# Pinning the first MLP blocks in order, splitting the last weights into dead tiles, and two moved products in a one-layer encoder kernel

## The chip, the cores and the metric

The kernel runs as one program on one core of a Trainium2 chip. The metric is device time of one launch, in microseconds (us), as the median of the runs shown. A core has five engines that each work through their own queue of instructions: TensorE (PE, with its weight loads shown apart as PEld), VectorE (DVE), ScalarE (ACT), GpSimd (POOL) and SyncE (SP), which issues nearly all DMAs here. They wait for each other through semaphores. The order of each queue is fixed when the program is built.

## The reference

One encoder layer over 256 tokens of width 2048, in float32. Only the last two parts bear on the change:

```python
h = rms_norm(x, norm_x_g[l]); mem_n = rms_norm(mem, norm_mem_g[l])
x = x + cross_attention(h, mem_n, w_xq[l], w_xkv[l], w_xo[l])      # ends in "... @ w_o"
h = rms_norm(x, norm_ffn_g[l])
x = x + jnp.square(jax.nn.relu(h @ w_ff1[l])) @ w_ff2[l]           # 2048 -> 8192 -> 2048
return rms_norm(x, norm_final_g)
```

## The kernel before

**Products in three parts.** A float32 operand is split into a high part, rounded to the fast matmul type (tiles `whi`, `whx` for weights, the first of a pair `q` for activations), and the rest (`wlo`, `wlx`). A product is high times high, high times low and low times high. Each 1 MB piece of weights goes through the same steps: a DMA from the SP queue into `raw` (three buffers), ACT copies half of it to the high tile (line 125), DVE subtracts to get the low tile (line 126), PE multiplies. There are three buffers of `whi` and `wlo`. From the MLP on, every fourth half goes into a fourth pair, `whx` and `wlx`, which lies in memory that the cross attention has given up and holds one buffer.

**Blocks.** A block (`blocks`, `blocks_in_steps`) makes 256 columns of a projection: it takes two pieces of weights and so four halves, a quarter of the depth each. A quarter is 16 matmuls: eight at line 210 (high half times both parts of the activations, 512 columns) and eight at line 211 (low half, 256 columns), into two banks of PSUM, `s0` and `s1` (two buffers each). At its end ACT and DVE add the parts up (`bo`, lines 220 and 221) and hand them to the caller.

**The end of the attention.** `residual_pass` multiplies by `w_xo` in eight blocks and adds to `rt`, the residual stream by features; it also collects the sum of squares in `acc2`. Its first two blocks are interleaved by quarters with `values()` of the last head, by a written list of which block takes the next step. When the eighth block is done, two tiny matmuls (line 1043) sum `acc2` over the partitions, DVE makes the mean of it (line 1045), POOL the inverse root (line 267), and DVE transposes the whole of `rt` into `tr` with four instructions (line 1123), so that it can be placed token by token into `res` by DMAs (`place`, line 1130).

**The MLP.** It runs in four parts of 2048 hidden columns (`fb` 0 to 3). Each part has a first projection, eight blocks of `w_ff1`, and a second, `with_seven`, which multiplies by 2048 rows of `w_ff2`; half of that is done with seven products in place of eight, on sums of tokens (`summed`) and of weights (`b11` to `b22`, loaded whole into the memory of `rt` and `tr`). Parts 1 to 3 are `early`: some of the seven products are made between blocks of the first projection. `read` notes a finished bank of PSUM that is to be added to `res`; `read_now` does so when the next product or `plain` piece starts (line 1141), and in the last part it also squares the sums for the final norm and multiplies by its gain (`settle`, line 1153). `product` splits its weights itself (lines 1234 and 1235) and may then overwrite one of the four weight tiles with a difference (line 1239).

**What sets the order.** A scheduler lays the instructions of each engine when the program is built, from priorities and a time model of its own. `issue_after` ties an instruction behind another. In parts 1 to 3 every quarter of a block is tied behind the one before it through the list `ends`; in part 0 it is not, and `None` is passed.

Of the kernel before, what the change touches and what calls it, by code (L numbers as in the profile page):

```python
# [18 lines left out]
D = 2048  # L19
# [33 lines left out]
def trunk(ctx: ExitStack, tc: tile.TileContext, x_f, mem_f, positions, lead_f, small_f, w_in, ret_gn_g, w_out, w_xq,  # L53
# [13 lines left out]
    def stream_ps():  # L67
        s0 = psp.tile([P, 512], F32, name="s0", tag="s0", bufs=2)
        s1 = psp.tile([P, 512], F32, name="s1", tag="s1", bufs=2)
        return s0, s1  # L70
# [8 lines left out]
    def half_tiles():  # L79

        turn[0] += 1
        if spare and turn[0] % 4 == 0:
            return tuple(spare[0].tile([P, 1024 + room], F32R, name=nm, tag=nm, bufs=1)
                         for nm, room in (("whx", 128), ("wlx", 0)))
        return tuple(wp.tile([P, 1024 + room], F32R, name=nm, tag=nm, bufs=3) for nm, room in (("whi", 64), ("wlo", 0)))
# [924 lines left out]
    def residual_pass(quads, w, gain, name, loader=None, between=None):  # L1010
        nxt = []
        acc = xa.tile([P, S], F32, name="acc2", tag="acc2", bufs=2)
        vec.memset(acc, 0.0)
        first_two = []
        for b2 in range(8):
            xc = loader(b2) if loader else None
            if b2 % 2 == 0:
                nxt.append(quad_b())

            def evac(b, ps, b2=b2, xc=xc):  # L1020
                k = 2 * b2 + b
                vec.tensor_add(rt[:, k, :], ps, xc[:, b, :] if loader else rt[:, k, :])
                g = gains[:, gain + k:gain + k + 1]
                qh, ql = (a[:, k % 4, :] for a in nxt[-1])
                act.activation(qh, rt[:, k, :], AF.Copy, scale=g)
                vec.scalar_tensor_tensor(ql, rt[:, k, :], g, qh.bitcast(F32), op0=ALU.mult, op1=ALU.subtract)
                sq = xa.tile([P, S], F32, name="sq2", tag="sq2", bufs=2)
                act.activation(sq, rt[:, k, :], AF.Square)
                vec.tensor_add(acc, acc, sq)

            if not between or b2 > 1:
                blocks(quads, w, b2 * 256, 2, evac)
                continue
            first_two.append(blocks_in_steps(quads, w, b2 * 256, 2, evac))
            if b2:
                for which in (0, 0, 0, None, 1, 0, 0, 1, 1, 1, 1):
                    if which is None:
                        between()
                    else:
                        next(first_two[which], None)  # L1040
        ps = bank()
        for t in range(NT):
            pe.matmul(ps[:, 2 * t:2 * t + 2], acc[:, t * P:(t + 1) * P], ones[:, :2], start=True, stop=True)
        s = sm.tile([P, NT], F32, name=f"{name}_s", tag="rc_s")
        vec.tensor_scalar(s, ps[:, 0:4:2], 1.0 / D, EPS, op0=ALU.mult, op1=ALU.add)
        r = cp.tile([P, NT], F32, name=f"{name}_r")
        rsqrt(r, s)
        return nxt, r
# [100 lines left out]
    def settle(n, t):  # L1149

        got = res[:, t, n * 512:(n + 1) * 512]
        square_sum(ssq4[:, t, (0, 1, 3, 2)[n]:(1, 2, 4, 3)[n]], got)
        vec.tensor_mul(got, got, final[0][:, n * 512:(n + 1) * 512])

    def mean_square(t):
        s = sm.tile([P, 1], F32, name="s4", tag="s4")
        vec.tensor_reduce(s, ssq4[:, t, 0:4], axis=AX.X, op=ALU.add)
        vec.tensor_scalar(s, s, 1.0 / D, EPS, op0=ALU.mult, op1=ALU.add)
        sums.append(s)
# [25 lines left out]
    def with_seven(hid, rows, last, early):  # L1185
# [3 lines left out]
        own = {}  # L1189
# [9 lines left out]
        def read(*those):  # L1199

            reads.extend(those)

        def read_now():
            for n, t, ps, *done in reads:
                add_later(n, t, ps)
                if last and done:
                    settle(n, t)
            reads.clear()

        def triple(o, lhs, rhs, key, last=False):  # L1210
# [13 lines left out]
                                 [a[:, i % 2, :] for a in halves[i // 2]], (n, t), q == 3 and i == 3)  # L1224
            ends.append(ins)

        def product(o, lhs, raw, key, then=None):


            halves = []  # L1230
            with tc.high_priority(offset=100000):
                for c in range(0, 2048, 1024):
                    hi, lo = (h[:, :1024] for h in half_tiles())
                    latest["hi"] = act.activation(hi, raw[:, c:c + 1024], AF.Copy).ins  # L1234
                    latest["lo"] = vec.tensor_sub(lo, raw[:, c:c + 1024], hi.bitcast(F32)).ins  # L1235
                    halves.append([a.rearrange("p (k n) -> p k n", n=512) for a in (hi, lo)])
                for c in range(0, 2048, 1024) if then else ():
                    with tc.issue_after(latest["lo"]):
                        vec.tensor_sub(*(a[:, c:c + 1024] for a in then))
            read_now()  # L1240
            for oc, k, c0, c1 in ([(a[:, :256], (key, c), c * 256, c * 256 + 256) for c, a in enumerate(o)]
                                  if isinstance(o, tuple) else [(o, key, 0, 512)]):
                for i in range(4):
                    ins = triple(oc, lhs(i), [a[:, i % 2, c0:c1] for a in halves[i // 2]], k, i == 3)
                ends.append(ins)

        def part(b, t):
            return lambda i: [a[:, 2 * (i % 2) + b, t * P:(t + 1) * P] for a in hid[i // 2]]

        def summed(j):  # L1250
            return lambda i: [a[:, i, j * P:(j + 1) * P] for a in s_hl]
# [5 lines left out]
        if early:  # L1257
# [13 lines left out]
            yield  # L1271
            product(shared, summed(2), b12, "shared", (b11, b21, b11))
            read((0, 1, shared), (1, 1, shared))
            yield
            for n in range(2):
                take(n, stream_ps())
# [2 lines left out]
            if last:  # L1279
                final.append(quad_a().both.rearrange("p k s -> p (k s)").bitcast(F32))  # L1280
                with tc.issue_after(fetched[-1]):
                    nc.sync.dma_start(final[0], norm_final_g.partition_broadcast(P))
            product(own[1][0], summed(3), b22, (1, 0))
            plain(0, 3)
            load_block(b22, 1, 3)
            product(own[0][0], part(1, 0), b21, (0, 0))
# [22 lines left out]
            read((3, 0, own[3][0], True), (3, 1, own[3][1]))  # L1309
            product(own[2][0], part(1, 0), b21, (2, 0))  # L1310
            read((2, 0, own[2][0], True))
            if last:
                read((2, 1, own[2][1]))
            product(shared, summed(2), b12, "shared")
            if last:
                mean_square(0)
                finish_row(0)
            read((2, 1, shared), (3, 1, shared, True))
            if not last:
                product(own[2][1], part(1, 1), b11, (2, 1))  # L1320
                read((2, 1, own[2][1]))
            else:
                ends_of = stream_ps()
                product(ends_of, part(1, 1), b11, "end")
                for c, ps in enumerate(ends_of):
                    got = add(2, 1, ps[:, :256], c * 256, c * 256 + 256)
                    junk = sm.tile([P, 512], F32, name="junk", tag="junk", bufs=1)
                    acc = ssq4[:, 1, 3 + c:4 + c]
                    vec.scalar_tensor_tensor(junk[:, :256], got, 1.0, got, op0=ALU.mult, op1=ALU.mult, accum_out=acc)
                    if c:  # L1330
                        vec.scalar_tensor_tensor(sums[1], acc, 1.0 / D, sums[1], op0=ALU.mult, op1=ALU.add)
                    else:
                        mean_square(1)
                finish_row(1)
# [40 lines left out]
    for fb in range(4):  # L1375
        hid = []
        rows = w_ff2[0, fb * D:(fb + 1) * D, :]
        early = fb > 0
        parts_of = with_seven(hid, rows, fb == 3, early)
        ends.clear()  # L1380
        for b2 in range(8):
            hs = fp.tile([P, 2, S], F32, name="hs", tag="hs", bufs=2)
            if b2 % 2 == 0:
                hid.append(quad_a())

            def evac_h(b, ps):
                if early:
                    act.activation(ps, ps, AF.Relu)
                    act.activation(hs[:, b, :], ps, AF.Square)
                else:  # L1390
                    vec.scalar_tensor_tensor(hs[:, b, :], ps, 0.0, ps, op0=ALU.max, op1=ALU.mult)
                qh, ql = (a[:, b2 % 2 * 2 + b, :] for a in hid[-1])
                act.activation(qh, hs[:, b, :], AF.Copy)
                vec.tensor_sub(ql, hs[:, b, :], qh.bitcast(F32))
                if b2 < 4 and b:
                    token_sums(b2, hs)

            blocks(h3, w_ff1[0], fb * D + b2 * 256, 2, evac_h, ends if early else None)
            if early and b2 > 2:
                next(parts_of)  # L1400
            if fb == 0:
                place(b2)
        for _ in parts_of:
            pass
# [42 lines left out]
```

## Time and profile before

| | |
|---|---|
| median of 3 runs | 2046.75 us (2046.49 to 2047.02) |
| profiled execution, its own time | 2046.86 us |
| its span, first to last instruction | 2045.2 us |
| mean granted TensorE clock | 0.999 |
| PE busy | 2033.4 us (99%) |
| DVE busy | 1550.1 us (76%) |
| ACT busy | 1185.1 us (58%) |
| DMA queue with the weights (q1) | 402.74 MB, 61.2% of 16 engines |

All times inside the profile are counted from the start of the span. The time of the run is 1.7 us longer than the span. PE's busy time covers nearly all of it, so the few places in which PE stands still, and the stretch behind its last matmul, are what a change of order can win or lose. In the views below a row of the timeline gives the start, the time taken, the engine, the line and operation, the tile written and those read, and, in brackets, how long the engine stood idle before it and which instruction ended that.

### The profile page before, as it was taken

The numbers are of one execution on the slowest core, as the hardware profiler recorded it, in microseconds if no ns is written. First come the engines' busy times: TensorE is split into PE (matmuls) and PEld (weight loads), VectorE is DVE, ScalarE is ACT, GpSimd is POOL, SyncE is SP. The second block draws the span as 40 slices with busy tenths as digits, with TensorE's granted clock in tenths as the row PEclk, the third lists the DMA queues.
The fourth block names the chain that finished last, engine by engine and source line by source line (L and its number), as shares of the span: only waits on it lengthen the run. The fifth ranks groups of instructions, "written<-read, shape, count | busy, mean of one in ns | idle before, by whom it ended". The sixth has DMA issues, their size and how long they took to land.

```text
span 2045.2 us, 28450 instructions
## 1 busy us (share of the span) xinstructions
PE 2033.4 (99%) x10802; PEld 1751.9 (86%) x10802; DVE 1550.1 (76%) x2422; ACT 1185.1 (58%) x1941; POOL 39.8 (2%) x50
## 2 busy tenths in 40 slices
PE   9999999999999999999999999999999999999998
PEld 7888888988888888888888899888888888888886
DVE  5887788779667875888567666777867887888788
ACT  6665764575457555755455555555546656656655
POOL 0000000000000000000000000000000000000000
PEclk9999999999999999999999999999999999999999
DMA  9689556455555655555467655569657646655761
GB/s 330 210 259 301 187 182 200 151 194 197 178 168 185 201 183 165 193 182 182 164 217 232 191 180 161 175 180 246 233 167 232 220 164 213 201 204 165 242 232 62
DMA packets 329225, 405.24 MB, mean 198 GB/s; under 512 B 34928, under 2 KB 239360, under 8 KB 328960
## 3 DMA queue, kind: packets, MB, share of 16 engines
q1 hardware_dynamic: 328656, 402.74, 61.2%
q8 instruction: 84, 1.38, 0.3%
q10 hardware_dynamic: 432, 0.69, 0.1%
q14 instruction: 53, 0.43, 0.1%
HBM read 389.74 MB, written 11.55 MB: 196 GB/s over the span
## 4 chain that ended last, share of the span: by engine, by line
PE 98%; DVE 1%; DMA 0%; ACT 0%; issue 0%; SPq 0%; POOLq 0%; POOL 0%; ACTq 0%
PE s L210 34%; PE s L211 18%; PE s L167 8%; PE s L168 8%; PE s L166 8%; PE s L1213 7%; PE b L1213 7%; PE s L403 1%; PE s L401 1%; PE s L402 1%; PE b L796 1%; PE b L699 1%; PE b L829 1%; PE b L138 0%; PE b L137 0%; PE b L139 0%
## 5 line engine op out<-in xcount | busy, mean ns | idle before, releaser
L210 PE MATMUL s<-q,whi 128*128 128x512 f32 x2816 | 973.3, 391 | 0.8 <-DVE bo L221 0.6
L126 DVE TENSOR_TENSOR wlo<-raw,whi 128x1024 fp32r<-128x1024 f32 x584 | 712.7, 1221 | 298.5 <-ACT whi L125 294.1
L125 ACT ACTIVATE whi<-raw 128x1024 fp32r<-128x1024 f32 x584 | 618.8, 1060 | 499.3 <-PE s L210 208.8
L211 PE MATMUL s<-q,wlo 128*128 128x256 f32 x2816 | 768.9, 281 | 0.0
L210 PEld LDWEIGHTS s<-q,whi 128*128 128x128 f32 x2816 | 520.7, 188 | 103.4 <-DVE bo L221 0.9
L211 PEld LDWEIGHTS s<-q,wlo 128*128 128x128 f32 x2816 | 528.9, 188 | 12.4 <-DVE wlo L126 0.4
L167 PE MATMUL s<-wlo,q 128*128 128x512 f32 x704 | 277.2, 394 | 0.0
L168 PE MATMUL s<-whi,q 128*128 128x512 f32 x704 | 274.9, 391 | 0.0
L166 PE MATMUL s<-whi,q 128*128 128x512 f32 x704 | 254.4, 391 | 0.0
L166 PEld LDWEIGHTS s<-whi,q 128*128 128x128 f32 x704 | 132.1, 188 | 27.3
L168 PEld LDWEIGHTS s<-whi,q 128*128 128x128 f32 x704 | 132.3, 188 | 26.2
L167 PEld LDWEIGHTS s<-wlo,q 128*128 128x128 f32 x704 | 132.3, 188 | 26.2
L220 ACT ACTIVATE bo<-s 128x256 f32<-128x256 f32 x192 | 73.2, 381 | 108.6 <-PE s L211 108.5
L221 DVE TENSOR_TENSOR bo<-bo,s 128x256 f32<-128x256 f32 x192 | 79.7, 415 | 46.5 <-ACT bo L220 46.0
L1235 DVE TENSOR_TENSOR wlo<-rt,whi 128x1024 fp32r<-128x1024 f32 x56 | 68.2, 1223 | 32.8 <-ACT whi L1234 32.0
L125 ACT ACTIVATE whx<-raw 128x1024 fp32r<-128x1024 f32 x60 | 63.6, 1060 | 46.5 <-PE s L1213 19.1
L210 PE MATMUL s<-q,whx 128*128 128x512 f32 x256 | 89.1, 389 | 0.0
L1213 PE MATMUL s<-whi,q 128*128 128x512 f32 (+1 forms) x280 | 88.8, 383 | 0.0
L126 DVE TENSOR_TENSOR wlx<-raw,whx 128x1024 fp32r<-128x1024 f32 x60 | 73.3, 1221 | 19.0 <-ACT whx L125 18.8
L1234 ACT ACTIVATE whi<-rt 128x1024 fp32r<-128x1024 f32 x56 | 59.3, 1060 | 39.6 <-PE s L1213 19.2
L1213 PE MATMUL b<-whi,q 128*128 128x512 f32 x220 | 71.5, 389 | 0.0
L211 PE MATMUL s<-q,wlx 128*128 128x256 f32 x256 | 70.4, 280 | 0.0
(344 smaller groups left out, 2373.0 us busy)
## 6 DMA issues: line engine op xcount, KB each, us to landing
raw<-w_in SPq DMA_DIRECT2D x143, 1024.0 KB
raw<-w_ff SPq DMA_DIRECT2D x100, 1024.0 KB
raw<-w_xkv SPq DMA_DIRECT2D x29, 1024.0 KB
raw<-w_out SPq DMA_DIRECT2D x16, 1024.0 KB
raw<-w_xq SPq DMA_DIRECT2D x16, 1024.0 KB
raw<-w_xo SPq DMA_DIRECT2D x16, 1024.0 KB
rt<-w_ff SPq DMA_DIRECT2D x14, 1024.0 KB
tr<-w_ff SPq DMA_DIRECT2D x14, 1024.0 KB
```

What stands on the lines that cost most here:

```text
L125: latest["hi"] = act.activation(hi[:, cs], src[:, cs], AF.Copy).ins
L126: latest["lo"] = vec.tensor_sub(lo[:, cs], src[:, cs], hi[:, cs].bitcast(F32)).ins
L166: pe.matmul(o, xh, wh, start=first, stop=False)
L167: pe.matmul(o, xh, wl, start=False, stop=False)
L168: pe.matmul(o, xl, wh, start=False, stop=last)
L210: pe.matmul(ps[b], lh, xhl, start=kk == 0, stop=False)
L211: ins = pe.matmul(ps[b][:, :S], ll, xh, start=False, stop=kk == KT - 1).ins
L220: act.activation(o, ps[b][:, S:], AF.Copy)
L221: vec.tensor_add(o, o, ps[b][:, :S])
L1213: ins = pe.matmul(o, lhs[l], rhs[r], start=key not in opened, stop=last and j == 2, skip_group_check=True).ins
L1234: latest["hi"] = act.activation(hi, raw[:, c:c + 1024], AF.Copy).ins
L1235: latest["lo"] = vec.tensor_sub(lo, raw[:, c:c + 1024], hi.bitcast(F32)).ins
```

## The change

Five edits, with no change in the number or size of matmuls:

1. Part 0 of the MLP gets the list `ends` as well, so that its blocks of the first projection are tied in order, as in the other parts.
2. In `residual_pass` the list of steps is `0, 0, 0, values, 1, 1, 0, 0, 1, 1, 1`: two quarters of the second block behind `values()` instead of one.
3. In the last part, the fifth of the seven products (`summed(3)` with `b22`) moves from the second projection to the end of the first. It goes to the bank `p5` instead of into `own[1][0]`, so that one more addition to `res` is needed.
4. In the last part, the splitting of weights is taken out of `product` into `parted`. The halves of the last two products, `b12` and `b11`, are both made before the last but one product; those of `b11` go into two tiles of `quad_b`, which held the activations of the first projection and are no longer read.
5. The bank (2, 1) is read a product earlier, and `settle` of (2, 0), `mean_square(0)` and `finish_row(0)` get a higher priority.

```diff
-                for which in (0, 0, 0, None, 1, 0, 0, 1, 1, 1, 1):
+                for which in (0, 0, 0, None, 1, 1, 0, 0, 1, 1, 1):
...
-                    settle(n, t)
+                    with tc.high_priority(offset=50000 if (n, t) == (2, 0) else 0):
+                        settle(n, t)
...
-        def product(o, lhs, raw, key, then=None):
+        def parted(raw, hold=None):
             halves = []
             with tc.high_priority(offset=100000):
                 for c in range(0, 2048, 1024):
-                    hi, lo = (h[:, :1024] for h in half_tiles())
+                    if hold:
+                        both = hold().both
+                        hi, lo = (both[:, a:a + 2, :].rearrange("p a s -> p (a s)") for a in (0, 2))
+                    else:
+                        hi, lo = (h[:, :1024] for h in half_tiles())
...
+        def product(o, lhs, raw, key, then=None, halves=None):
+            halves = halves or parted(raw)
...
             product(shared, summed(2), b12, "shared", (b11, b21, b11))
             read((0, 1, shared), (1, 1, shared))
+            if last:
+                product(p5, summed(3), b22, "p3")
+                read((1, 0, p5))
             yield
...
-            product(own[1][0], summed(3), b22, (1, 0))
+            if not last:
+                product(own[1][0], summed(3), b22, (1, 0))
...
+                read((2, 1, own[2][1]))
+                of_7, of_4 = parted(b12), parted(b11, quad_b)
+                product(shared, summed(2), None, "shared", halves=of_7)
+                with tc.high_priority(offset=50000):
+                    mean_square(0)
+                    finish_row(0)
+                read((2, 1, shared), (3, 1, shared, True))
                 ends_of = stream_ps()
-                product(ends_of, part(1, 1), b11, "end")
+                product(ends_of, part(1, 1), None, "end", halves=of_4)
...
-            blocks(h3, w_ff1[0], fb * D + b2 * 256, 2, evac_h, ends if early else None)
+            blocks(h3, w_ff1[0], fb * D + b2 * 256, 2, evac_h, ends)
```

How the queues of the engines change is seen in the order of the built programs. The numbers are those of tiles: `s0_13017` and `s1_13018` are the banks of the MLP's first block, `s0_13127` and `s1_13128` those of its second; `whi_13063` and `wlo_13064` are the first block's third quarter of weights, `whx_13067` and `wlx_13068` its fourth; `whi_13131`, `whi_13135` and `whi_13173` with their `wlo` are the second block's first three.

On PE, where the `w_xo` blocks end and the MLP begins, before: behind the third quarter of the first block stands the second block, and the first block's fourth quarter comes later (its first two matmuls near the end of the second block's second quarter, the other fourteen behind that block's third).

```order
L211 MATMUL s1_13018<-q_12575,wlo_13064 128x256
L210 MATMUL s0_13127<-q_12127,whi_13131 128x512
L211 MATMUL s0_13127<-q_12127,wlo_13132 128x256
L210 MATMUL s1_13128<-q_12127,whi_13131 128x512
L211 MATMUL s1_13128<-q_12127,wlo_13132 128x256
L210 MATMUL s0_13127<-q_12127,whi_13131 128x512
L211 MATMUL s0_13127<-q_12127,wlo_13132 128x256
L1043 MATMUL b_12993<-ones_75,acc2_12125 128x2 x2
L210 MATMUL s1_13128<-q_12127,whi_13131 128x512
```

The same place on PE, now:

```order
L211 MATMUL s1_13018<-q_12575,wlo_13064 128x256
L1043 MATMUL b_12993<-ones_75,acc2_12125 128x2 x2
L210 MATMUL s0_13017<-q_12784,whx_13067 128x512
L210 MATMUL s1_13018<-q_12784,whx_13067 128x512
L211 MATMUL s0_13017<-q_12784,wlx_13068 128x256
L211 MATMUL s1_13018<-q_12784,wlx_13068 128x256
L210 MATMUL s0_13017<-q_12784,whx_13067 128x512
```

The sums of `acc2` and the whole fourth quarter have moved in front of the second block. On DVE at the same place, before:

```order
L126 TENSOR_TENSOR wlo_13136<-raw_13129,whi_13135 128x1024
L126 TENSOR_TENSOR wlo_13174<-raw_13171,whi_13173 128x1024
L1045 TENSOR_SCALAR n3_s_12996<-b_12993 128x2
L1123 STREAM_TRANSPOSE tr_13007<-rt_10152 128x1024 x4
L126 TENSOR_TENSOR wlx_13068<-raw_13061,whx_13067 128x1024
L1114 TENSOR_TENSOR rstd3q_13000<-n3_r_12998 128x2
```

And now:

```order
L126 TENSOR_TENSOR wlo_13136<-raw_13129,whi_13135 128x1024
L1045 TENSOR_SCALAR n3_s_12996<-b_12993 128x2
L1123 STREAM_TRANSPOSE tr_13007<-rt_10152 128x1024 x4
L126 TENSOR_TENSOR wlo_13174<-raw_13171,whi_13173 128x1024
L1114 TENSOR_TENSOR rstd3q_13000<-n3_r_12998 128x2
L126 TENSOR_TENSOR wlx_13068<-raw_13061,whx_13067 128x1024
```

The mean and the four transposes stand one place earlier, the low half of the fourth quarter two places later, still behind the transposes. The third place is the end of the program, on DVE: `tr` and `rt` are here the memory of `b12`, `b21`, `b11` and `b22`, and the tiles `q_18773` and `q_18776` of the second fence are the dead ones of `quad_b`. Before:

```order
L126 TENSOR_TENSOR wlo_18707<-raw_18704,whi_18706 128x1024
L126 TENSOR_TENSOR wlx_18711<-raw_18704,whx_18710 128x1024
...
L1235 TENSOR_TENSOR wlx_18769<-rt_10152,whx_18768 128x1024
L1141 SCALAR_TENSOR_TENSOR res_13006<-b_18465,rstd3q_13000,res_13006 128x512
L1153 TENSOR_TENSOR res_13006<-res_13006,q_18324 128x512
L1141 SCALAR_TENSOR_TENSOR res_13006<-b_18464,rstd3q_13000,res_13006 128x512
L1235 TENSOR_TENSOR wlo_18805<-rt_10152,whi_18804 128x1024
L1235 TENSOR_TENSOR wlo_18809<-rt_10152,whi_18808 128x1024
L1153 TENSOR_TENSOR res_13006<-res_13006,q_18324 128x512
```

And now:

```order
L126 TENSOR_TENSOR wlo_18708<-raw_18705,whi_18707 128x1024
L1238 TENSOR_TENSOR q_18773<-rt_10152,q_18773 128x1024
L126 TENSOR_TENSOR wlx_18712<-raw_18705,whx_18711 128x1024
L1238 TENSOR_TENSOR q_18776<-rt_10152,q_18776 128x1024
L1141 SCALAR_TENSOR_TENSOR res_13006<-b_17779,rstd3q_13000,res_13006 128x512
L1141 SCALAR_TENSOR_TENSOR res_13006<-b_18466,rstd3q_13000,res_13006 128x512
L1238 TENSOR_TENSOR wlo_18741<-tr_13007,whi_18740 128x1024
...
L1238 TENSOR_TENSOR wlx_18770<-rt_10152,whx_18769 128x1024
L1141 SCALAR_TENSOR_TENSOR res_13006<-b_18465,rstd3q_13000,res_13006 128x512
L1153 TENSOR_TENSOR res_13006<-res_13006,q_18345 128x512 x2
```

The two splits for the last product (`wlo_18805` and `wlo_18809` before, the two `q` tiles now) stand eight and nine rows earlier, and the addition of one bank has moved up with them. The order of the `w_xo` stage is the same as before on all five engines (only the numbers of some tiles differ).

More of the change, by code (lines that the diff above doesn't have):

```diff
@@ L1236, in product @@
                     halves.append([a.rearrange("p (k n) -> p k n", n=512) for a in (hi, lo)])
+            return halves
+        def product(o, lhs, raw, key, then=None, halves=None):
+            halves = halves or parted(raw)
+            with tc.high_priority(offset=100000):
                 for c in range(0, 2048, 1024) if then else ():
@@ L1311, in with_seven @@
             read((2, 0, own[2][0], True))
[L1312 to L1318, printed above, removed]
             if not last:
+                product(shared, summed(2), b12, "shared")
+                read((2, 1, shared), (3, 1, shared))
                 product(own[2][1], part(1, 1), b11, (2, 1))
```

## The prediction

> **What bounds the kernel now.** I read the page first: busy times, then the chain that ended last.
>
> ```profile
> PE 2033.4 (99%) x10802; PEld 1751.9 (86%) x10802; DVE 1550.1 (76%) x2422; ACT 1185.1 (58%) x1941; POOL 39.8 (2%) x50
> PE 98%; DVE 1%; DMA 0%; ACT 0%; issue 0%; SPq 0%; POOLq 0%; POOL 0%; ACTq 0%
> ```
>
> TensorE is busy 99% of the span and 98% of the chain is its own work. The edits neither add nor remove a matmul. So the time changes only by what PE stands still, and by the stretch behind its last matmul. Next, PE's waits, of which these belong to the stages that change:
>
> ```profile
> PE s L210 <- DVE bo L221: 0.6, 1, 0.6
> PE s L210 <- DVE q L134: 0.3, 1, 0.3
> PE s L1213 <- DVE wlo L126: 0.2, 1, 0.2
> PE s L1213 <- DVE wlo L1235: 0.2, 1, 0.2
> ```
>
> All that PE waits there is 1.3 us, and some more by the starts of its matmuls, as shown below. This is all that a better order can win on PE; a worse order can lose any amount, since nothing behind it has slack to give back. That asymmetry decides the case.
>
> **The first MLP blocks (edit 1).** PE around the first block's third quarter, in the timeline:
>
> ```profile
> 1358.78 0.39 PE L210 MATMUL s<-q,whi 128*128 128x512 f32 x1
> ...
> 1359.81 0.50 PE L1043 MATMUL b<-ones,acc 128*128 128x2 f32 x4
> 1360.17 0.47 PE L210 MATMUL s<-q,whi 128*128 128x512 f32 x1
> ...
> 1370.26 0.28 PE L211 MATMUL s<-q,wlx 128*128 128x256 f32 x1
> 1371.12 0.50 PE L210 MATMUL s<-q,whi 128*128 128x512 f32 x1 [0.58 <-DVE bo L221]
> ```
>
> 1358.78 is the first matmul of the second block, put in front of the sums at line 1043. At 1370.26 the first block's fourth quarter ends, and the third block has to wait for its bank. Matmuls of this kind start 0.12 us apart, so 0.86 - 0.12 = 0.74 us are lost, and 0.11 more in the first one behind it (0.50 instead of 0.39): 0.85 us. With the blocks in order this goes, since the third block then starts a whole quarter of the second later.
>
> What comes in its place is read from DVE and ACT at the same time:
>
> ```profile
> 1357.52 1.23 DVE L126 TENSOR_TENSOR wlo<-raw,whi 128x1024 fp32r<-128x1024 f32 x1 [1.09 <-ACT whi L125]
> ...
> 1361.14 0.15 DVE L1045 TENSOR_SCALAR n_s<-b 128x2 f32<-128x2 f32 x1
> 1361.21 4.62 DVE L1123 STREAM_TRANSPOSE tr<-rt 128x1024 f32<-128x1024 f32 x4
> 1365.75 1.18 DVE L126 TENSOR_TENSOR wlx<-raw,whx 128x1024 fp32r<-128x1024 f32 x1
> ...
> 1366.92 1.22 DVE L126 TENSOR_TENSOR wlo<-raw,whi 128x1024 fp32r<-128x1024 f32 x1
> ```
>
> ```profile
> 1358.91 1.06 ACT L125 ACTIVATE whi<-raw 128x1024 fp32r<-128x1024 f32 x1 [1.42 <-PE s L210]
> 1360.35 1.06 ACT L125 ACTIVATE whx<-raw 128x1024 fp32r<-128x1024 f32 x1 [0.38 <-PE b L1043]
> 1364.78 2.01 ACT L125 ACTIVATE whi<-raw 128x1024 fp32r<-128x1024 f32 x2 [3.36 <-DMA raw<-w_ff]
> ```
>
> The low half `wlx` of the first block's fourth quarter had its input at 1361.41 (ACT row, 1360.35 + 1.06) but was made at 1365.75, behind four transposes that take 4.62 us. Before, PE covers this with three quarters of the second block. Now the fourth quarter is next, and on DVE `wlx` stands behind the transposes and one more split. Step by step, with the clock of the old trace:
>
> - The sums of line 1043 move to 1358.78. They hold PE for 1360.17 - 1359.81 = 0.36 us. ACT followed them by 1360.35 - 1359.81 = 0.54; DVE's line 1045, free since 1358.75 (1357.52 + 1.23), should follow alike, at 1359.32.
> - From there to the end of the transposes, where the next split starts, it takes 1365.75 - 1361.14 = 4.61: 1363.93. Then the split `wlo_13174` and line 1114 with their pace of 1366.92 - 1365.75 = 1.17: 1365.10. Then `wlx`, 1.2: 1366.30.
> - The high half is earlier: ACT's row at 1358.91 ends at 1359.97, `whx` follows and is done at 1361.0. So PE does the two high matmuls at 1361.0 and stands until about 1366.35.
> - Without a wait PE would want `wlx` at 1358.78 + 0.36 + 2 x 0.23 = 1359.60. It stands 6.75 us, and 0.11 in the restart: 6.9.
>
> Net of the 0.85 that goes: **+6.0 us**. All later work shifts with it. Bounds: 5.0 if line 1045 starts at once and every transpose takes no longer than a plain 1.0; 6.5 if the semaphores of the three steps cost 0.2 each. I take 6.0, as all durations are from this place. Nothing later gives it back: the windows show one quarter (16 matmuls) taking 2.77 us and three taking 8.28, with PE busy throughout.
>
> ```profile
> 1350.50:1358.78 8.28, 8.28 (x50) 7.33 (x49) 6.65 (x11) 5.04 (x9) 0.00 (x0) 1.00 0.45 128
> 1356.01:1358.78 2.77, 2.77 (x18) 2.45 (x17) 1.65 (x3) 1.06 (x1) 0.00 (x0) 1.00 0.01 3
> ```
>
> The later blocks need a fourth half once in 4 x 2.77 = 11 us, three quarters after its buffer came free, 8.3 us for 2.3 us of work on ACT and DVE: no wait.
>
> **The clock of PE.** PE's two high matmuls end at about 1361.6, and it then stands for 4.75 us at a stretch. The old trace has such a gap only in its tail, and matmuls at half pace only at its start:
>
> ```profile
> 2036.19:2039.70 3.51, 0.00 (x0) 0.00 (x0) 2.77 (x11) 3.45 (x7) 0.88 (x2) 1.00 0.45 165
> 2039.72:2045.20 5.48, 0.00 (x0) 0.00 (x0) 0.60 (x2) 0.79 (x2) 0.00 (x0) 0.50 0.75 274
> ```
>
> ```profile
> 4.33 0.77 PE L401 MATMUL s<-whi,q 128*128 128x256 f32 x2 [0.29 <-DVE q L336]
> 5.59 0.40 PE L401 MATMUL s<-whi,q 128*128 128x256 f32 x2
> ```
>
> The clock fell to 0.50 some 3.5 us after the last matmul; at the start, 4.3 us into the span, two matmuls still took 0.77 instead of 0.40, at 5.6 no longer. So it may fall in the new gap, last for some 4 to 5 us behind it and cost half of that: 0 to 2.4. I take 0.5, near the lower end, since the pause is little longer than those 3.5 us and the fall has to come before its end. [...]
>
> **`w_xo` (edit 2).** PE waits here for the last head's values:
>
> ```profile
> 1278.07 0.28 PE L139 MATMUL b<-pth,vvl 128*128 128x256 f32 x1
> 1278.61 0.50 PE L210 MATMUL s<-q,whi 128*128 128x512 f32 x1 [0.26 <-DVE q L134]
> ```
>
> This is 0.42 us plus 0.11. One more quarter in between would hide it, but the order of all engines in this stage is what it was: the scheduler had put it so already. 0.0, and the wait stays.
>
> **The fifth product (edit 3)** changes places with a `plain` piece, with its splits in the same slots. It adds one addition to `res` on DVE, 0.74 us (row at 2022.81 below), soon covered by idle time such as this:
>
> ```profile
> 1976.28 1.23 DVE L1235 TENSOR_TENSOR wlo<-rt,whi 128x1024 fp32r<-128x1024 f32 x1 [1.49 <-ACT whi L1234]
> ```
>
> 0.0; 0.74 at most without that cover.
>
> **The end (edits 4 and 5).**
>
> ```profile
> 2013.86 0.50 PE L1213 MATMUL s<-wlo,q 128*128 128x512 f32 x1 [0.17 <-DVE wlo L126]
> ...
> 2031.44 0.39 PE L1213 MATMUL b<-wlx,sh 128*128 128x512 f32 x1
> ...
> 2032.58 0.28 PE L1213 MATMUL s<-whi,q 128*128 128x256 f32 x1
> ...
> 2033.90 0.39 PE L1213 MATMUL s<-wlo,q 128*128 128x256 f32 x1 [0.16 <-DVE wlo L1235]
> ...
> 2035.91 0.28 PE L1213 MATMUL s<-whi,q 128*128 128x256 f32 x1
> ```
>
> ```profile
> 2022.81 0.74 DVE L1141 SCALAR_TENSOR_TENSOR res<-b,rstd3q,res 128x512 f32<-128x512 f32 x1
> ...
> 2025.71 1.23 DVE L1235 TENSOR_TENSOR wlo<-rt,whi 128x1024 fp32r<-128x1024 f32 x1 [1.03 <-ACT whi L1234]
> ...
> 2028.43 1.22 DVE L1235 TENSOR_TENSOR wlx<-rt,whx 128x1024 fp32r<-128x1024 f32 x1 [0.18 <-ACT whx L1234]
> ...
> 2031.50 2.35 DVE L1235 TENSOR_TENSOR wlo<-rt,whi 128x1024 fp32r<-128x1024 f32 x2
> ...
> 2035.81 0.90 DVE L1141 SCALAR_TENSOR_TENSOR res<-s,rstd3q,res 128x256 f32<-128x256 f32 x2
> ```
>
> The last product has 24 matmuls, 2032.58 to 2035.91, 23 steps in 3.33 us. From 2033.90 on, 16 steps take 2.01, with 0.11 for the restart: 0.119 each. Without waits 23 x 0.119 = 2.73: 0.6 saved. DVE's two splits (2.35 from 2031.50) go up into the stretch before, with an addition: about 2.9 us, of which 1.2 fall into its idle time (1.03 and 0.18). So the `wlx` of 2028.43 ends 1.7 later, at about 2031.3, and PE's first matmul with it starts at 2031.44: just in time, or up to 0.4 late. In exchange DVE is free when the last bank is done, and the final norm and the output follow PE's end as now. **-0.6 us** (bounds -1.0 and 0). The wait at 2013.86 stays; the rows before it stand as they did.
>
> **The sum** is against the profiled execution, 2046.86 us (span 2045.2 and 1.7 around it), 0.1 above the median: 6.0 + 0.5 + 0 + 0 - 0.6 = +5.9, or 2052.7; against the median **2052.6 us**.
>
> **The rivals.**
>
> *The transposes are quick when PE is still.* They run beside matmuls that read the same memory in the old trace; alone, they may take less. The point is 4.1 us of net loss (0.2%, what a measurement can tell from no change): transposes of 2.8 instead of 4.62 us give +4.1 and end within it, at 2050.8 or less. Against it: they are DVE's own work at 1.16 us for 1024 elements, no slower than the splits at 1.22. Chance 0.10.
>
> *The clock falls for long,* with 1 to 2.4 us in place of 0.5: 2053.1 to 2054.5. For it, the gap is longer than the 3.5 us of the tail. 0.27.
>
> *The queue of SP.* Behind the transposes it now issues four and then eight placing DMAs in one go, ahead of the fourth block's weights.
>
> ```profile
> 1372.64 4.82 SPq L1130 DMA_DIRECT2D res<-tr  x4
> 1378.75 7.27 SPq L1130 DMA_DIRECT2D res<-tr  x7
> ```
>
> At 1.04 to 1.2 us each, eight take 8.3 to 9.6: and the four ahead of them end by 1363.93 + 4.8 = 1368.7: the load is issued at 1377 to 1378.3. The load that ACT waited for at 1364.78 stood there for 3.36 us; with twice that and 2.3 for the split it is ready at 1386 to 1387.3. PE takes up the fourth block at 1366.35 + 2.4 (rest of the quarter) + 8.28 + 2.77 + 11.05 = 1390.9. Only a load of over 10 us would be late; three us of that give 2055.6. 0.07.
>
> *The change wins its waits and nothing is lost,* if something makes `wlx` early after all: 0.85 + 0.6 gone, 2045.3, within 0.2%. With the rest unknown, 0.04.
>
> **How the numbers follow.** The forecast (net 4.1 to 6.4 us, 2050.9 to 2053.2) has 0.52. With the clock's and SP's cases that is 0.86 slower; the first rival and most of the last are the same, 0.11; faster 0.03. The range, 2050.2 to 2055.5, takes in the clock's bound and part of the outer cases.
>
> **What would show it.** In the new profile: PE still for about 5 us at 1361 to 1366, ended by DVE's `wlx` of line 126; line 1045 at about 1359.3, the transposes right behind; no wait at 1371 or in the last product; the wait at 1278 as before. Wrong if PE's longest wait there is under 3 us, or if a wait for `raw` shows up near 1391 to 1397.

## The result, and the profile after

The changed kernel takes **2054.7 us** (median of six runs, 2053.9 to 2056.17); the kernel before took 2046.66 in the same comparison (six runs, 2046.27 to 2048.55). The ratio is 1.0039, with a 95% interval of 1.0028 to 1.005: slower by 8.0 us, where 5.9 were forecast and the range went up to 2055.5. The profiled execution is the slowest of the six, 2056.17 us with a span of 2054.5.

PE's waits on the page of the changed kernel, in the answer that lists them (what waits, for what, us in total, times, longest):

```profile
PE s L211 <- DVE wlx L126: 4.7, 1, 4.7
PE s L210 <- ACT whx L125: 1.7, 1, 1.7
...
PE s L210 <- DVE q L134: 0.3, 1, 0.3
```

The two at the top are new. The wait for the bank at the third block (`bo`, 0.6 before) and that for the last product's `wlo` are gone; the small one at the last `w_xo` quad is as it was. None is for a transfer. The timeline of PE at that quad and at the first blocks of the MLP:

```profile
1280.32 0.50 PE L210 MATMUL s<-q,whi 128*128 128x512 f32 x1 [0.26 <-DVE q L134]
...
1360.56 0.50 PE L1043 MATMUL b<-ones,acc 128*128 128x2 f32 x4
1362.75 0.73 PE L210 MATMUL s<-q,whx 128*128 128x512 f32 x2 [1.69 <-ACT whx L125]
1368.16 0.79 PE L211 MATMUL s<-q,wlx 128*128 128x256 f32 x2 [4.68 <-DVE wlx L126]
1368.75 0.63 PE L210 MATMUL s<-q,whx 128*128 128x512 f32 x1
1369.18 0.41 PE L211 MATMUL s<-q,wlx 128*128 128x256 f32 x1
1369.39 0.63 PE L210 MATMUL s<-q,whx 128*128 128x512 f32 x1
...
1371.31 0.46 PE L210 MATMUL s<-q,whx 128*128 128x512 f32 x1
```

and of DVE:

```profile
1361.10 0.16 DVE L1045 TENSOR_SCALAR n_s<-b 128x2 f32<-128x2 f32 x1 [0.57 <-PE b L1043]
1361.18 4.61 DVE L1123 STREAM_TRANSPOSE tr<-rt 128x1024 f32<-128x1024 f32 x4
1365.72 1.18 DVE L126 TENSOR_TENSOR wlo<-raw,whi 128x1024 fp32r<-128x1024 f32 x1
1366.82 0.15 DVE L1114 TENSOR_TENSOR rstd3q<-n_r 128x2 f32<-128x2 f32 x1
1366.89 1.22 DVE L126 TENSOR_TENSOR wlx<-raw,whx 128x1024 fp32r<-128x1024 f32 x1
```

and of ACT:

```profile
1360.69 1.06 ACT L125 ACTIVATE whi<-raw 128x1024 fp32r<-128x1024 f32 x1 [1.42 <-PE s L210]
1361.66 1.04 ACT L125 ACTIVATE whx<-raw 128x1024 fp32r<-128x1024 f32 x1
```

So on both engines the operand that PE needs next stands behind others: `wlx` behind the four transposes, a split and line 1114, and `whx` directly behind another high half. (Over the whole of DVE's queue `wlx` moved back by one place; the section on the change counts two.)

Line 1043 was forecast at 1358.78 and stands at 1360.56. These 1.78 us are no part of the change: this launch is late already at the `w_xo` wait (1280.32 for 1278.61 before), which fits its being the slowest of the six. With 1.78 taken off, line 1045 stands at 1359.32, the transposes end at 1363.94, PE goes on at 1366.38: forecast were 1359.32, 1363.93 and 1366.35.

Behind the wait, a pair of matmuls takes 0.64 us (1368.75 to 1369.39) instead of 0.345. The windows, each half as long as the 6.83 us that the half clock lasted, show why. A row has the stretch, its length, the busy us of PE, PEld, DVE, ACT and POOL with their counts, then the granted clock, the share of the DMA engines and GB/s:

```profile
1361.19:1364.60 3.41, 0.73 (x2) 0.30 (x2) 3.41 (x5) 1.51 (x2) 0.70 (x1) 1.00 0.69 202
1364.60:1368.01 3.41, 0.00 (x0) 0.00 (x0) 3.41 (x5) 0.00 (x0) 0.00 (x0) 0.50 0.46 127
1368.01:1371.42 3.41, 3.26 (x11) 2.88 (x12) 0.09 (x1) 0.00 (x0) 0.00 (x0) 0.50 0.78 129
1371.43:1374.84 3.41, 3.41 (x22) 2.99 (x20) 2.40 (x5) 1.91 (x4) 0.00 (x0) 1.00 1.04 274
```

The clock was halved at 1364.60 and came back at 1371.43. At the end of the program, PE's last product in the timeline:

```profile
2041.68 3.04 PE L1214 MATMUL s<-q 128*128 128x256 f32 x24
```

It took 3.61 before (2032.58 to 2036.19): 0.57 gained. The parts, all from the profiled executions:

| part | forecast | measured | from |
|---|---|---|---|
| PE stands at the first block's fourth quarter | +6.9 | +6.78 | 1360.56 to 1368.16 is 7.60; 0.36 + 2 x 0.23 without waits |
| matmuls at half pace | +0.5 | +1.5 | 1368.16 to 1371.31 is 3.15; 2 x 0.12 + 4 x 0.345 at full pace |
| third block's wait gone | -0.85 | -0.85 | no wait there |
| last product | -0.6 | -0.57 | above |
| from PE's last matmul to the end | 0 | +0.7 | 2054.45 - 2044.72 = 9.7 (the span is 2054.5 when rounded); before 2045.2 - 2036.19 = 9.0 |
| sum | +5.9 | +7.6 | |

As a cross-check, from line 1043 to PE's end it took 684.16 us now and 676.38 before. Before, seven matmuls of the second block (1.03 us) stood ahead of that line; now they stand behind it. Without them it is 6.75 longer, where the first four parts give 6.86. The median differs by 8.0; the 0.4 that is left has no part of its own and is within what single launches differ by.

### The profile page after: what moved, and what is told of

It is laid out like the page before. It is cut to its first block, busy times and chain, and to the rows that moved or that the text cites. A ratio compares the mean times of both kernels' runs of the same rounds, so it can differ in the third digit from the quotient of the medians.

```text
span 2054.5 us, 28452 instructions
## 1 busy us (share of the span) xinstructions
PE 2035.4 (99%) x10802; PEld 1753.1 (85%) x10802; DVE 1551.2 (76%) x2423; ACT 1184.6 (58%) x1941; POOL 38.6 (2%) x50
## 4 chain that ended last, share of the span: by engine, by line
PE 95%; DVE 2%; DMA 1%; issue 0%; ACT 0%; SPq 0%; POOLq 0%; POOL 0%; ACTq 0%; DVEq 0%
PE s L210 34%; PE s L211 18%; PE s L167 8%; PE s L168 8%; PE s L166 8%; PE b L1214 7%; PE s L1214 7%; DMA raw<-w_xkv 1%; PE b L796 1%; PE b L699 1%; PE b L829 1%; PE b L138 0%; DVE wlo L1238 0%; PE b L137 0%; PE b L139 0%; DVE wlo L126 0%
## 5 line engine op out<-in xcount | busy, mean ns | idle before, releaser
L168 PE MATMUL s<-whi,q 128*128 128x512 f32 x704 | 274.9, 391 | 0.0
L166 PE MATMUL s<-whi,q 128*128 128x512 f32 x704 | 254.4, 391 | 0.0
L1214 PE MATMUL s<-whi,q 128*128 128x512 f32 x272 | 88.0, 389 | 0.0
```

The source lines that it names most:

```text
L166: pe.matmul(o, xh, wh, start=first, stop=False)
L168: pe.matmul(o, xl, wh, start=False, stop=last)
L1214: ins = pe.matmul(o, lhs[l], rhs[r], start=key not in opened, stop=last and j == 2, skip_group_check=True).ins
```

## The experiments

Each is compared with the kernel before on its own chip; runs of the kernel before scattered there from 2046.3 to 2049.7, so that single differences below 1 us are read from the traces. Where a stretch is given as "from line 1043 to PE's end", it is what no difference at the start touches. Even this stretch scatters: in two launches with the same order on PE (edits 2 to 5, with the final norm's weights in one piece and in eight) it is 676.42 and 675.93 us, so that differences below some 0.5 us in it show nothing.

**Edit 1 alone, and everything but edit 1.**

```diff
-            blocks(h3, w_ff1[0], fb * D + b2 * 256, 2, evac_h, ends if early else None)
+            blocks(h3, w_ff1[0], fb * D + b2 * 256, 2, evac_h, ends)
```

> The kernel before with edit 1 alone (the blocks of part 0 tied by `ends`). Theory: nearly all of the loss is here. From the trace of the changed kernel: 1.91 us of wait for `whx`, 4.85 for `wlx`, 1.3 for matmuls at half pace behind them, less the 0.86 at the third block: +7.2, so 2053.9 us, with a clock of about 0.997. Rival: edit 1 costs the forecast 6.0 and the rest of the 8.0 comes from the edits at the end: 2052.7 or less.

> The changed kernel without edit 1, so edits 2 to 5 alone. Theory: the last product no longer waits (-0.54), and the stretch behind PE's last matmul is 0.7 longer, as in the trace of the changed kernel: 2046.8 us; if that 0.7 belongs to the one launch and not to the program, 2046.1. Rival: the edits at the end cost one or two us that the trace of one launch hides: 2047.7 to 2048.7.

Edit 1 alone: ratio 1.0036 (1.0024 to 1.0049), median 2056.29 against 2048.2, or +8.1, with the same two waits of 1.69 and 4.68. The theory had +7.2, the rival +6.0. Edits 2 to 5: ratio 1.0 (0.9991 to 1.0009). So edit 1 carries the whole loss, and the others come out at nothing: in their trace the last product takes 3.03 us, but the stretch behind PE's end is again 9.64. The rival with one or two us lost at the end is out.

**The transposes later: all four, and two of them.** In the changed kernel, behind the first block (the loop that issued them ahead of it keeps none, or two):

```diff
...
+                for c in range(0, 4) if b2 == 0 else ():   # range(2, 4) for two
+                    with tc.issue_after(latest["lo"]):
+                        flip(c)                            # the vec.transpose of before
                 place(b2)
...
```

> The changed kernel with the four transposes of `rt` issued behind the split `wlx` of the first block instead of ahead of it; nothing is left out. [...] Rival: `wlx` is late for another reason (its input, or the memory that it is written to), and the transposes only fill the time: 2054.7.

> The changed kernel with two of the four transposes issued behind `wlx`, two ahead of it. Theory: each transpose ahead of `wlx` costs PE its own 1.15 us, no more and no less, so the wait for `wlx` is 2.5 (with four 4.85, with none 0.96); and the clock falls in this launch too, since PE is busy for well under half of the window in which the waits lie (1.9 and 2.5 of idle time around 0.6 of matmuls): 2052.4 us on a chip where the changed kernel takes 2054.7. [...]

PE's line 1043 and its wait for `wlx` in the timelines, first with all four later, then with two:

```profile
1357.87 0.50 PE L1043 MATMUL b<-ones,acc 128*128 128x2 f32 x4
...
1361.57 0.79 PE L211 MATMUL s<-q,wlx 128*128 128x256 f32 x2 [0.79 <-DVE wlx L126]
```

```profile
1358.14 0.50 PE L1043 MATMUL b<-ones,acc 128*128 128x2 f32 x4
...
1363.48 0.80 PE L211 MATMUL s<-q,wlx 128*128 128x256 f32 x2 [2.14 <-DVE wlx L126]
```

From line 1043 to the first matmul with `wlx` PE takes 7.60 us with four transposes ahead of `wlx`, 5.34 with two (1358.14 to 1363.48) and 3.70 with none (1357.87 to 1361.57). One pair costs its own 2.3 (2.26), the other 1.64, since without it the split that is next on DVE waits for ACT (0.52):

```profile
1359.09 1.23 DVE L126 TENSOR_TENSOR wlo<-raw,whi 128x1024 fp32r<-128x1024 f32 x1 [0.52 <-ACT whi L125]
```

The transposes in DVE's queue account for 3.90 of the 4.68; the rival is out. The 0.79 that stays is the split that makes `wlx` (1.22 us), which starts at 1360.30 behind another one. In time, four later: ratio 1.0019 (1.001 to 1.0028), median +3.7; the changed kernel's +8.0 less the 3.90 would be +4.1. Two later, one run: 2051.7, or +4.05 on its chip, where the text on record has +5.7. The clock fell in both traces:

```profile
1357.24:1360.65 3.41, 1.73 (x11) 1.26 (x10) 2.32 (x5) 2.00 (x2) 0.69 (x1) 1.00 0.42 86
1360.66:1364.07 3.41, 2.62 (x9) 2.21 (x9) 3.41 (x4) 0.00 (x0) 0.00 (x0) 0.50 1.00 302
1364.07:1367.48 3.41, 3.41 (x13) 2.92 (x12) 2.73 (x4) 1.72 (x3) 0.00 (x0) 0.50 0.73 234
```

These are windows of the kernel with four later. It fell behind a window in which PE was busy for 1.73 of 3.41 us (with two later also 1.73, 1357.17 to 1360.58), and did not come back behind one with 2.62. So in this launch the small wait of 1.69 alone stood ahead of the fall. And the fall was dearer here: until the clock came back at 1367.48, matmuls stood where the changed kernel has its wait. From 1361.57 on they ran at half clock for 5.91 us, in the changed kernel for 3.27 (1368.16 to 1371.43). By its loss, 1.5 in 3.15 us, an estimated 2.8 was lost here. From line 1043 to PE's end this launch took 682.0 us, only 2.2 less than the changed kernel, although its wait is 3.9 shorter. Not every launch need have fallen: five of its eleven runs had a mean clock of 0.997 and a mean time of 2053.1, the other six 0.998 or 0.999 and 2051.4. That is a rough sign only, since the moment at which the full clock first came, 5.37 us into the span in the kernel before and 6.09 in the changed one, moves the mean too.

**PE kept busy in the wait.**

```diff
...
+                    for _ in range(18):
+                        with tc.issue_after(ins):
+                            ins = pe.matmul(spot, wh[:, 0, cut[0]], xhl, start=True, stop=True).ins
...
```

> The changed kernel with 18 extra matmuls of 128x512 into an unused bank, between PE's two high matmuls of the fourth quarter and the first low one: they fill the wait for `wlx` (18 x 0.23 = 4.1 of 4.85 us) and end before it does. [...] Rival: the half pace comes from something else (the transfers or the splits that run beside it): 2054.7.

```profile
1362.17 0.72 PE L210 MATMUL s<-q,whx 128*128 128x512 f32 x2 [1.69 <-ACT whx L125]
1362.74 4.35 PE L213 MATMUL b<-q,whx 128*128 128x512 f32 x18
1367.59 0.50 PE L216 MATMUL s<-q,wlx 128*128 128x256 f32 x2 [0.50 <-DVE wlx L126]
```

The wait is as long as it was and the matmuls behind it go at full pace (a pair in 0.34 us, 1367.93 to 1368.27). From line 1043 to PE's end it is 1.5 us less than in the changed kernel. Ratio 1.0026 (1.0016 to 1.0035), median +5.6. The half pace is the clock's, and it costs 1.5. Two of the nine runs still had a mean clock of 0.997; no trace tells whether it fell in them. The window with the wait of 1.69 held more matmuls in this launch, and the clock stayed:

```profile
1358.50:1361.91 3.41, 1.99 (x14) 1.74 (x12) 2.61 (x4) 1.99 (x3) 0.70 (x1) 1.00 0.20 53
```

**The 0.7 us behind PE's end.** In the program with edits 2 to 5, the final norm's weights come in eight pieces; and the kernel before gets edit 3 alone.

```diff
-                    nc.sync.dma_start(final[0], norm_final_g.partition_broadcast(P))
+                    for c in range(0, D, D // 8):
+                        nc.sync.dma_start(final[0][:, c:c + D // 8], norm_final_g[c:c + D // 8].partition_broadcast(P))
```

> Edits 2 to 5 with the final norm's weights loaded in eight pieces. It is to tell why the programs with edits 3 to 5 take 9.64 to 9.74 us from PE's last matmul to the end, and the others 9.02. Theory: in them an 8 KB packet of the instruction queue starts 6.2 us behind PE's last matmul, among the packets of the output, and the last packets end at 8.15 instead of 7.64; SyncE has one instruction more than before, which moves its step to a new block of code there. With nine more instructions the packet comes before the output: none between 1.4 and 8.2 us behind PE's last matmul, and a stretch of 9.0 to 9.1. Rival 1: the packet is another engine's: it stays at 6.2, and the stretch at 9.6 to 9.7. Rival 2: the packet goes, the stretch stays, and the order of the final rows is the cause.

> The kernel before with edit 3 alone (the fifth product in the first projection). Theory: no new wait, 676.1 us from line 1043 to PE's end as before; all that edit 3 does is to add instructions. It has as many on VectorE as the changed kernel (two more than before) and as many on SyncE (one more): if the place of the 8 KB packet hangs on these counts, it starts at about 6.2 us behind PE's end and the stretch is 9.6 to 9.7. Rival: the packet hangs on the splits and the final rows of edits 4 and 5: it stays at 9.7, and the stretch at 9.0.

The windows of the output's last 0.9 us, from 7.4 us behind PE's end on; the last number of a row is GB/s. Changed kernel, then eight pieces:

```profile
2052.12:2052.42 0.30, 0.00 (x0) 0.00 (x0) 0.00 (x0) 0.00 (x0) 0.00 (x0) 0.50 0.07 27
2052.42:2053.02 0.60, 0.00 (x0) 0.00 (x0) 0.00 (x0) 0.00 (x0) 0.00 (x0) 0.50 0.05 17
```

```profile
2043.10:2043.40 0.30, 0.00 (x0) 0.00 (x0) 0.00 (x0) 0.00 (x0) 0.00 (x0) 0.50 0.00 0
2043.40:2044.00 0.60, 0.00 (x0) 0.00 (x0) 0.00 (x0) 0.00 (x0) 0.00 (x0) 0.50 0.00 0
```

In the changed kernel a few packets trickle on at 27 and 17 GB/s, with a share of 0.07 and 0.05, which is about one of the 16 DMA engines; with eight pieces all is done. The DMA view of the changed kernel from 2050.90 to 2051.20, in the midst of its output, has the packet of the instruction queue:

```profile
q10 hardware_dynamic: 30, 0.06, 52.7%
q1 hardware_dynamic: 26, 0.05, 47.1%
q14 instruction: 1, 0.01, 6.5%
```

With eight pieces it comes 0.1 us behind PE's end, ahead of the output, and the stretch is 8.84. With edit 3 alone it starts 6.4 us behind PE's end, and the stretch is 9.78, although the end's code is that of before; PE's part is the same within the scatter (676.6 us from line 1043 to its end). These two are one launch each, and by its time of 2047.05 us (2047.24 for the kernel before on its chip) the second can't be told from before. But the traces go the same way: with the packet among the output the stretch is 9.7 in the changed kernel, where it starts 6.2 us behind PE's end, and 9.78 with edit 3 alone; with none there it is 9.0 in the kernel before, where the packet comes behind the span, and in the one with the tie below (none from 1.4 to 8.3 us behind PE's end), and 8.84 with eight pieces. So the seemingly free edit 3 goes with 0.7 us at the end: one experiment put the packet among the output, the other took it out, and the 0.7 came and went with it. How a packet that takes 0.31 us would make the output end 0.5 to 0.7 later is not shown. Whose packet it is stays open, and that it is a block of SyncE's code is not shown either. The kernel with the tie below has as many instructions on SyncE as the changed kernel (920), and there none came among the output, so SyncE's count alone does not decide. VectorE's count in the built programs does sort these five: with 3104 or 3105 instructions (before, the tie) no packet is among the output, with 3106 it starts at 6.2 and 6.4, with 3107 (eight pieces) at 0.1. But no run changes VectorE's number alone, so this is a sign and no proof.

**Edit 2 made to take effect.** The blocks of `w_xo` get a list `ends` of their own:

```diff
-            first_two.append(blocks_in_steps(quads, w, b2 * 256, 2, evac))
+            first_two.append(blocks_in_steps(quads, w, b2 * 256, 2, evac, tied))
```

> Edits 2 to 5, with the first two `w_xo` blocks tied in the order of the list (by a list `ends` of their own), so that edit 2 takes effect: two quarters of the second block behind `values()`. Theory: the wait of 0.43 us for the last quad goes, but 24 matmuls of the second block no longer stand inside and ahead of `values()`, where they covered its waits; PE waits there for 1 to 4 us instead: slower than edits 2 to 5 without the tie by 0.5 to 3.5 us. Rival: `values()` has its inputs in time, and the tie gains 0.5 us.

One run of 2046.9 (2047.65 for the kernel before on its chip). The theory was wrong: PE got no new wait at `values()`, and the entry for `q` of line 134 left the list of PE's waits; the start that was 0.43 us late is still 0.26 late. So the rival's sign, at 0.17 instead of 0.5.

**Can the change be had without its loss?** Three versions: (a) edits 2 to 5, the transposes behind `wlx`, the norm in eight pieces; (b) the whole change, but with `whx` and `wlx` taken from the new pool only from the second block on, and eight pieces; (c) the same with the tie.

```diff
-    spare.append(fp)
...
             if fb == 0:
+                if not b2:
+                    spare.append(fp)
                 place(b2)
```

> Blocks of part 0 in the order of before (edit 1 undone), the four transposes issued behind `wlx`, the other edits as changed, and the final norm's weights loaded in eight pieces instead of one, which adds nine instructions to SyncE's program. Theory: the wait at the third block goes (-0.86), since the first block's last quarter ends 13 matmuls earlier; the last product does not wait (-0.54); the stretch behind PE's last matmul is 9.0 again instead of 9.7: 1.4 us faster than before (ratio 0.9993). Rival: DVE's addition of line 221 stays behind two splits and is as late as it was, so that the third block still waits: 0.5 faster (0.9997).

> The whole change, with the pool of the spare halves `whx` and `wlx` used only from the second MLP block on (so that the first block's fourth quarter is not written into memory that line 1043 still reads), and the final norm's weights in eight pieces. Theory: edit 1 loses only because that quarter hangs on line 1043 and stands behind the transposes; now it is made ahead of both, so that PE has neither the wait of 1.9 nor that of 4.85 nor the fall of the clock; the wait at the third block (0.86) and that in the last product (0.54) are gone, and the stretch behind PE is 8.8: 1.6 us faster than before (ratio 0.9992). Rival: with three buffers in place of four PE waits for one in the first block, 1 to 3 us: 1.000 to 1.0007.

> As the kernel with the spare halves from the second block on, and the first two `w_xo` blocks tied in the order of their list. Theory: another 0.2 us, as the tie alone took the wait of 0.43 down to 0.26: 1.8 us faster than before in all (ratio 0.9991). Rival: no difference between the two, as runs scatter by more than 0.2 us.

Ratios: (a) 0.9993 (0.9984 to 1.0002), (b) 0.9994 (0.9985 to 1.0003), (c) 0.9996 (0.9987 to 1.0005). The medians are 1.1, 0.6 and 0.7 us below the kernel before, where 1.4, 1.6 and 1.8 were expected, and none can be told from it by time. By the traces the waits go as expected. In (a) PE has no wait at all in the blocks of the MLP's first projection, 1.5 us less from line 1043 to its end, and 8.84 behind it. In (b) both long waits of edit 1 and the fall of the clock are gone, with one small wait there, for a `wlo` of the second block:

```profile
1370.03 0.51 PE L211 MATMUL s<-q,wlo 128*128 128x256 f32 x2 [0.24 <-DVE wlo L126]
```

So the tie of the blocks does no harm where the halves of the fourth quarter are made ahead of line 1043 (PE then does six of its sixteen matmuls ahead of that line). In the changed kernel they were late because they lie in the memory of the closed `xattn` pool, which line 1043 is the last to read, so that both engines have them behind it in their queues: `whx` behind another high half on ACT, `wlx` behind the transposes, which line 1045 lets go first. The wait for line 1043 itself is not what ends last in the trace: `whx` started at 1361.66, when ACT was free, and DVE had gone on behind line 1043 at 1361.10.

## Why the prediction was right, and where it was off

- **What bounds the kernel, and the sign**: held. The time changed by PE's waits and the stretch behind it.
- **Edit 1, +6.0 net**: held to 0.1 us, step for step, the wait for `whx` included. The step that carried it, transposes and a split ahead of `wlx`, was shown by taking the transposes away in two doses (3.9 of the 4.68).
- **The clock, +0.5**: mis-sized; it was 1.5. Two reasons were given for the low end, that the pause was little longer than 3.5 us and that the fall had to come before its end. Both treat a fall as something that needs PE to be wholly still. The fall came 1.1 us after the end of PE's last matmul (1363.48) and 3.6 ahead of the end of the wait, behind a window of 3.41 us with 0.73 us of matmuls; with the transposes later it came behind one with 1.73. And all six runs of the changed kernel had a mean clock of 0.996 or 0.997, all five of edit 1 alone 0.997, against 0.998 and 0.999 in the runs of before, which fits a fall in every launch. The bound of 0 to 2.4 held the 1.5. The rival "the clock falls for long" (0.27), whose low end of 1 was the author's estimate, is what happened.
- **Edit 2, 0.0**: held; the wait of before is there unchanged.
- **Edit 3, 0.0**: the step that failed. Its addition on DVE cost nothing, as said, but with its instructions a packet of the instruction queue came to lie among the output, 6.2 us behind PE's end: 0.7.
- **Edits 4 and 5, -0.6**: held on PE (-0.57): the last product's splits stand eleven and ten rows earlier (the section on the change has eight and nine), and PE did not wait for the `wlx` that they push back. That "the final norm and the output follow PE's end as now" did not, for the reason of edit 3.
- **The sum**: 2.1 us too low. The clock (1.0) and the end (0.7) erred the same way, and 0.4 has no part of its own. 2054.7 lies above the band 2050.9 to 2053.2, which had the best chance, and within the range only because that made room for a clock that falls for long; for a longer end no term and no rival stood.
- **The rivals**: the transposes were not quicker with PE still (4.61 against 4.62 us). No wait for `raw` at the fourth block. Nothing was made early.

## What to carry to other kernels

Where an order is tied by hand, look at what the producer's engine has queued ahead of the operand that the tie now needs first, and at whose memory that operand is written into: here a tie worth 0.85 us met 5.8 us of queue. A pause of PE can cost more than itself: with the transposes later, 1.68 us of idle time in a window of 3.41 stood ahead of a halved clock, and a shorter wait saves less than its length when the half clock then falls on busy matmuls (here 2.2 us of 3.9). With a chain that is 98% one engine, an edit that only reorders can win the few waits in the list and no more, and an added instruction is not always free (here edit 3 went with 0.7 us by the traces).

## What the runs showed of the hardware

- PE's granted clock in the changed kernel was full from 6.09 us, 0.50 from 1364.60, full from 1371.43 and 0.50 from 2047.27; in the kernel before it was full from 5.37 and 0.50 from 2039.71. The stretches at full clock, 1358.51, 675.84 and 2034.34 us, are within 0.1 us of 199, 99 and 298 times the 6.827 us at half clock.
- Cut into windows of 3.41 us that end where the clock changes, the falls came behind a window in which PE was busy for 0.73 us (changed kernel) and 1.73 (four transposes later, and two later), and behind PE's last matmul for 0.87 (changed kernel, 2043.85 to 2047.26) and 0.00 (before, 2036.30 to 2039.71). One with 1.99 (PE kept busy in the wait, 1358.50 to 1361.91) was followed by no fall. At half clock, windows with 2.62 us (four later) and 1.27 (two later, 1360.59 to 1364.00) did not bring it back; one with 3.26 (changed kernel) and one with 3.41 (four later) did.
- A single 8 KB packet of the instruction queue among the last 2.1 MB of output goes with a longer stretch behind PE's end: 9.7 us in the changed kernel and 9.78 with edit 3 alone, against 9.0 before and with the tie, and 8.84 with eight pieces, where none is among the output.
